# Nine products of constants ahead of the first operands, a first load on another queue, and the last statistics on another engine

## The chip, the cores and the metric

The kernel runs on one core of a Trainium2 chip. The metric is the device time of one execution in microseconds (us). "Before" is the median of three runs; one execution of the same kernel was recorded with a profile. TensorE (PE) multiplies matrices, VectorE (DVE), ScalarE (ACT) and GpSimd (POOL) work element by element, SyncE (SP) issues nearly all the transfers (DMA).

## The reference, cut to what matters

The kernel computes one decoder layer for 1024 tokens of width 2048, in float32: an RMS norm, one input projection of 9224 columns, two groups of recurrent heads in chunked form, an output projection with a residual, a gated per-layer embedding, and a last RMS norm. The change touches the first load of x, the first products, and the end:

```python
u = rmsnorm(h, norm_w[l])
proj = jnp.einsum('bsd,dc->bsc', u, w_in[l])
...
h = h + jnp.einsum('bsc,cd->bsd', y, w_out[l])
e = jnp.einsum('bsr,rd->bsd', p[l], w_pe[l])
gate = jax.nn.sigmoid(jnp.einsum('bsd,de->bse', rmsnorm(h, pe_norm_w[l]), w_pg[l]))
h = h + gate * e
out = rmsnorm(h, final_norm_w)   # h * rsqrt(mean(h*h) + EPS) * w
```

## The kernel before, in words

The tokens are worked in two halves of 512. Every large product is made in three passes (`mm3`, lines 253 to 255): each operand is split into a high part and a rest, and high x high, high x rest and rest x high are added up in PSUM. A weight piece `raw` comes by DMA, ACT casts the high part (L119), DVE takes the rest (L120); three pieces are kept ahead of the products. For the first half, x comes transposed in tiles of two k rows each (`xt`), ACT makes the high part of u (L240) from it and the norm weights in `vec_sb`, DVE the rest (L241). So the first block of products needs, for each k from 0 to 15, both parts of u and of its weights.

At the start SP issues, in this order: the first half of the first x tile (L75), the vector of constants `vec_sb` (L76), then weight parts (L167) and x tiles (L222, L224) in turn. ACT begins with loading its function table and makes `ones_r`, a rounded copy of the constant matrix `ones` (L86), which DVE has filled (L84). A program that lays out the order of the instructions on each engine works from simulated times (`schedule_with_timeline_sim=True`), so instructions don't all stand in the order of the source.

At the end `gate_block` makes the last column block (cb = 3) of the second half: token tiles 0 and 1 first, then 2 and 3 (prefix "b"), and the last token tile in two halves of 256 columns. For each piece ACT takes the sigmoid (L785), DVE multiplies by the embedding (L786) and adds the residual (L792), ACT squares and sums (L795) into a column of `ss3`. After the second half of a token tile DVE adds the five columns (L800), scales and adds EPS (L124), POOL raises to -1/2 (L125, `rstd_of`), ACT scales column blocks 0 and 2 (L809), DVE 1 and 3 (L807, L805), and SP issues the four stores of 256 KB each (L810).

Of the kernel before, what the change touches and what calls it, by code (L numbers as in the profile page):

```python
# [16 lines left out]
F32 = mybir.dt.float32  # L17
# [3 lines left out]
AF = mybir.ActivationFunctionType  # L21
ALU = mybir.AluOpType
AX = mybir.AxisListType

P = 128
S = 1024
D = 2048
KT = D // P
HT = 512
NC = HT // P  # L30
EPS = 1e-6
# [5 lines left out]
NMASK = 3 + len(LEVELS)  # L37
WIDE = (10, 16, 24)
HOLD = 2
LATE = [f"bg1_3_{pc}" for pc in (1, 3, 5, 7)]  # L40

V_NORM, V_PEN, V_MLN, V_HGN, V_LB, V_CW, V_CB, V_END = 0, 16, 32, 40, 48, 64, 96, 104
# [3 lines left out]
def hybrid_layer(ctx: ExitStack, tc, x, xT, pT, w_blk, w_v0, w_vw, w_out, w_pg, w_pe, vec, gb, fnw,  # L46
                 ident_in, causal_in, lmask_in, out):
    nc = tc.nc
# [9 lines left out]
    small = ctx.enter_context(tc.tile_pool(name="small", bufs=3))  # L58
    pj = ctx.enter_context(tc.tile_pool(name="pj", bufs=4, space=PS))
    mx = ctx.enter_context(tc.tile_pool(name="mx", bufs=4, space=PS))  # L60
# [5 lines left out]
    def psj(name):  # L66
        return pj.tile([P, 512], F32, tag="pj", name=name)

    def psm(name):
        return mx.tile([P, 512], F32, tag="mx", name=name)  # L70
# [1 line left out]

    vec_sb = const.tile([P, V_END], F32, name="vec_sb")
    x0 = mix.tile([P, 2, HT], F32, tag="at", name="xt0_0")
    nc.sync.dma_start(out=x0[:, 0], in_=xT[0:P, 0:HT])  # L75
    nc.sync.dma_start(out=vec_sb, in_=vec)  # L76
    ident = const.tile([P, P], F32, name="ident")
    causal = const.tile([P, P], F32, name="causal")
# [2 lines left out]
    neghalf = const.tile([P, 8], F32, name="neghalf")  # L81
    nc.vector.memset(neghalf, -0.5)
    ones = const.tile([P, P], F32, name="ones")
    nc.vector.memset(ones, 1.0)  # L84
    ones_r = orpool.tile([P, P + 112], F32R, name="ones_r")[:, 0:P]
    nc.scalar.copy(out=ones_r, in_=ones)  # L86

# [34 lines left out]
    def rstd_of(ss, n, width, name, tag="rstd"):  # L122
        r = small.tile([P, width], F32, tag=tag, name=name)
        nc.vector.tensor_scalar(out=r, in0=ss, scalar1=1.0 / n, scalar2=EPS, op0=ALU.mult, op1=ALU.add)  # L124
        nc.gpsimd.tensor_tensor(out=r, in0=r, in1=neghalf[:, 0:width], op=ALU.pow)  # L125
        return r
# [24 lines left out]
    def next_piece(between=None):  # L151
        nm, src = w_order[len(w_tiles)]
        n = src.shape[1] * src.shape[2]
        raw = wpool.tile([P, WP], F32, tag="wraw", name=f"raw_{nm}")[:, 0:n]
        if nm in LATE:
            hl = [upool.tile([P, 2, HT], F32R, tag="u", name=f"hl_{nm}_{i}") for i in range(2)]
# [16 lines left out]
    def load_piece(name):  # L173

        while len(w_tiles) < len(w_order) and (len(w_tiles) < AHEAD or w_order[len(w_tiles) - AHEAD][0] != name):
            next_piece()
        return dict(w_tiles[-AHEAD - 4:])[name]
# [74 lines left out]
    def mm3(ps, ah, al, bh, bl, first, last):  # L252
        nc.tensor.matmul(ps, lhsT=ah, rhs=bh, start=first, stop=False)  # L253
        nc.tensor.matmul(ps, lhsT=ah, rhs=bl, start=False, stop=False)  # L254
        nc.tensor.matmul(ps, lhsT=al, rhs=bh, start=False, stop=last)  # L255
# [432 lines left out]
    for half in range(2):  # L688
# [14 lines left out]
        for cb in range(4):  # L703
# [10 lines left out]
            for t in range(NC):  # L714
                tt = half * NC + t
# [5 lines left out]
                jk = tl.tile([P, 512], BF16, tag="junk2", bufs=1, name=f"jk2{half}_{cb}_{t}")  # L721
# [3 lines left out]
            for j in range(4):  # L725
                k = cb * 4 + j
                pt = psm(f"pht{half}_{k}")
                for t in range(NC):
# [5 lines left out]
                                               op0=ALU.mult, op1=ALU.subtract)  # L734
# [4 lines left out]
        ss3 = small.tile([P, NC, 5], F32, tag="ss3", bufs=1, name=f"ss3_{half}")  # L739
        nc.vector.memset(ss3, 0.0)  # L740
        h2 = [[None] * 4 for t in range(NC)]
        def gate_block(cb, ts_, pref):

            cs = slice(cb * 512, (cb + 1) * 512)
            wpe = load_piece(f"{pref}e{half}_{cb}")
            pe_sb = {}
            for t in ts_:
                pe = psm(f"pe{half}_{cb}_{t}")
                for kk in range(2):
                    ts = slice(kk * HT + t * P, kk * HT + (t + 1) * P)  # L750
                    sl = slice(kk * 512, (kk + 1) * 512)
                    mm3(pe, pp[:, 0, ts], pp[:, 1, ts], wpe[:, 0, sl], wpe[:, 1, sl], kk == 0, kk == 1)
                pe_sb[t] = pe

            units = []
            for t in ts_:
                parts = 2 if pref == "b" and t == NC - 1 else 1
                w = 512 // parts
                units += [(t, slice(i * w, (i + 1) * w), psj(f"pg{half}_{cb}_{t}_{i}")) for i in range(parts)]
            hold = HOLD if pref == "b" else 8  # L760
            hls = []
            for pc in range(8):
                hl = load_piece(f"{pref}g{half}_{cb}_{pc}")
                for kk in range(2):
                    sl = slice(kk * 512, (kk + 1) * 512)
                    hls.append([hl[kk][:, i] if isinstance(hl, list) else hl[:, i, sl] for i in range(2)])
                if pc < hold:
                    order = [(pc * 2 + kk, un) for kk in range(2) for un in units]
                elif pc == 7:
                    order = [(k, un) for un in units for k in range(2 * hold, KT)]  # L770
                else:
                    continue
                for k, (t, cl, ps) in order:
                    ts = slice(t * P, (t + 1) * P)
                    mm3(ps[:, cl], hns[k][:, 0, ts], hns[k][:, 1, ts], hls[k][0][:, cl], hls[k][1][:, cl],
                        k == 0, k == KT - 1)
            fb = tl.tile([P, 512], F32, tag="fb", bufs=1, name=f"fb{pref}{half}_{cb}")
            nc.sync.dma_start(out=fb, in_=fnw[:, cs].broadcast_to([P, 512]))
            for t, cl, ps in units:
                tt = half * NC + t  # L780
                if cl.start == 0:
                    hr = xh.tile([P, 512], F32, tag="xr", name=f"hr{half}_{cb}_{t}")
                    nc.sync.dma_start(out=hr, in_=h_dram[tt][:, cs])
                    gt = xh.tile([P, 512], F32, tag="ht", name=f"gt{half}_{cb}_{t}")
                nc.scalar.activation(out=gt[:, cl], in_=ps[:, cl], func=AF.Sigmoid, scale=r2[:, t:t + 1])  # L785
                nc.vector.tensor_tensor(out=gt[:, cl], in0=pe_sb[t][:, cl], in1=gt[:, cl], op=ALU.mult)  # L786
                if h2[t][cb] is None:
                    h2t = upool.tile([P, 2, HT], F32, tag="u", name=f"h2_{half}_{cb}_{t}")
                    c0 = cb - cb % 2
                    h2[t][c0], h2[t][c0 + 1] = h2t[:, 0], h2t[:, 1]  # L790
                hh = h2[t][cb]
                nc.vector.tensor_tensor(out=hh[:, cl], in0=gt[:, cl], in1=hr[:, cl], op=ALU.add)  # L792
                jk = tl.tile([P, 512], BF16, tag="junk2", bufs=1, name=f"jk3{half}_{cb}_{t}_{cl.start}")
                col = cb + (cl.start > 0)
                nc.scalar.activation(out=jk[:, cl], in_=hh[:, cl], func=AF.Square, accum_out=ss3[:, t, col:col + 1])  # L795
                if cb < 3:
                    nc.vector.tensor_tensor(out=hh, in0=hh, in1=fb, op=ALU.mult)
                elif cl.stop == 512:
                    s1 = small.tile([P, 1], F32, tag="s1", name=f"s1_{half}_{t}")
                    nc.vector.tensor_reduce(out=s1, in_=ss3[:, t], axis=AX.X, op=ALU.add)  # L800
                    r3 = rstd_of(s1, D, 1, f"r3_{half}_{t}")
                    for c in range(4):
                        ho = h2[t][c]
                        if c == 3:
                            nc.vector.scalar_tensor_tensor(out=ho, in0=ho, scalar=r3, in1=fb, op0=ALU.mult, op1=ALU.mult)  # L805
                        elif c == 1:
                            nc.vector.tensor_scalar(out=ho, in0=ho, scalar1=r3, scalar2=None, op0=ALU.mult)  # L807
                        else:
                            nc.scalar.activation(out=ho, in_=ho, func=AF.Copy, scale=r3)  # L809
                        nc.sync.dma_start(out=out[tt * P:(tt + 1) * P, c * 512:(c + 1) * 512], in_=ho)  # L810

        for cb in range(4):
            if half == 1 and cb == 3:
                gate_block(cb, (0, 1), "a")
                gate_block(cb, (2, 3), "b")
            else:
                gate_block(cb, range(NC), "")
# [81 lines left out]
```

## Time and profile before

| what | value |
|---|---|
| median of 3 runs | 2372.8 us (2372.53 to 2372.96) |
| the profiled execution | 2372.51 us, span 2370.5 us |
| PE busy | 2355.8 us, 99% of the span |
| DVE, ACT, POOL busy | 1170.9, 765.8, 66.3 us |
| granted TensorE clock, mean | 0.999 |
| DMA | 287.42 MB, mean 121 GB/s |

The span runs from the first instruction to the last on the profile's clock; the execution's time has 2.0 us around it. In rows of the timeline the columns are start, duration, engine, line, operation, output and inputs, shape, and how often; in brackets stands how long the engine had been idle and what released it. A matmul's recorded duration contains its way through the array: the step from one start to the next is what it costs in a row of them.

### The profile page before, as it was taken

The page shows a single profiled execution, that of the slowest core. Times are in us where ns is not written, and L with a number is a line of the kernel's source. Part 1 is how long each engine was busy: PE and PEld are TensorE (multiplying, and loading weights), DVE is VectorE, ACT ScalarE, POOL GpSimd, SP SyncE. Part 2 cuts the span into 40 slices and gives each one's busy share as a digit, 9 for nine tenths or more (in the row PEclk, how much of TensorE's full clock was granted, in tenths as well). Part 3 has the DMA queues.
Part 4 walks back from the last instruction along what each step waited for, and adds up shares of the span by engine and source line. Part 5 has one row for each costly group of instructions (what it writes and reads, how often), then busy time and mean ns, then how long its engine had stood idle before and what let it go on. Part 6 is the DMA issues. An engine that isn't in the chain of part 4 may idle for free.

```text
span 2370.5 us, 28577 instructions
## 1 busy us (share of the span) xinstructions
PE 2355.8 (99%) x11548; PEld 1984.1 (84%) x11548; DVE 1170.9 (49%) x1657; ACT 765.8 (32%) x1211; POOL 66.3 (3%) x96
## 2 busy tenths in 40 slices
PE   9999999999999999999999999999999999999998
PEld 7898888888888898988888888888888888888887
DVE  6655254265556857343534563675433444333336
ACT  6433232222222434232322222241423334332235
POOL 0000000000000000000000000000000000000000
PEclk9999999999999999999999999999999999999999
DMA  8433332322222423333333222343444456444436
GB/s 322 140 99 107 97 101 87 107 82 88 83 96 90 151 72 116 92 113 98 99 115 98 80 82 88 89 147 125 138 125 133 133 157 221 140 153 134 120 117 217
DMA packets 93452, 287.42 MB, mean 121 GB/s; under 512 B 10872, under 2 KB 11640, under 8 KB 93320
## 3 DMA queue, kind: packets, MB, share of 16 engines
q1 hardware_dynamic: 88200, 268.82, 36.5%
q0 software_dynamic: 5120, 16.78, 1.8%
q8 instruction: 90, 1.47, 0.3%
q14 instruction: 42, 0.34, 0.0%
HBM read 260.36 MB, written 25.20 MB: 120 GB/s over the span
## 4 chain that ended last, share of the span: by engine, by line
PE 99%; DMA 0%; DVE 0%; SPq 0%; ACT 0%; issue 0%; ACTq 0%; POOLq 0%
PE pj L254 15%; PE pj L253 15%; PE pj L255 15%; PE pt L253 5%; PE pt L255 5%; PE pt L254 5%; PE po L253 5%; PE pg L253 5%; PE po L255 5%; PE pg L254 5%; PE po L254 5%; PE pg L255 5%; PE pl L594 2%; PE pe L255 1%; PE pe L254 1%; PE pe L253 1%
## 5 line engine op out<-in xcount | busy, mean ns | idle before, releaser
L253 PE MATMUL pj<-u,hl 128*128 128x512 f32 x1536 | 603.5, 394 | 5.3 <-ACT hl L119 5.3
L254 PE MATMUL pj<-u,hl 128*128 128x512 f32 x1536 | 602.4, 392 | 0.1
L255 PE MATMUL pj<-u,hl 128*128 128x512 f32 x1536 | 601.2, 392 | 0.0
L120 DVE TENSOR_TENSOR hl<-raw,hl 128x1024 fp32r<-128x1024 f32 (+2 forms) x259 | 313.7, 1212 | 449.2 <-ACT hl L119 448.4
L119 ACT CAST hl<-raw 128x1024 fp32r<-128x1024 f32 (+2 forms) x259 | 269.4, 1040 | 819.8 <-PE pj L255 554.1
L253 PEld LDWEIGHTS pj<-u,hl 128*128 128x128 f32 x1536 | 288.8, 188 | 64.8 <-ACT hl L119 5.3
L254 PEld LDWEIGHTS pj<-u,hl 128*128 128x128 f32 x1536 | 289.1, 188 | 59.9 <-DVE u L241 0.9
L255 PEld LDWEIGHTS pj<-u,hl 128*128 128x128 f32 x1536 | 289.0, 188 | 59.6 <-issue 0.2
L254 PE MATMUL pt<-hl,u 128*128 128x512 f32 (+2 forms) x640 | 223.7, 350 | 0.0
L253 PE MATMUL pt<-hl,u 128*128 128x512 f32 (+2 forms) x640 | 222.9, 349 | 0.5 <-DVE raw L385 0.5
L255 PE MATMUL pt<-hl,u 128*128 128x512 f32 (+2 forms) x640 | 221.9, 348 | 0.0
L253 PE MATMUL po<-hl_o,ys 128*128 128x512 f32 x512 | 200.5, 393 | 0.0
L254 PE MATMUL po<-hl_o,ys 128*128 128x512 f32 x512 | 200.0, 391 | 0.0
L255 PE MATMUL po<-hl_o,ys 128*128 128x512 f32 x512 | 199.4, 390 | 0.0
L253 PE MATMUL pg<-hl_g,hnt 128*128 128x512 f32 x448 | 174.9, 390 | 0.0
L254 PE MATMUL pg<-hl_g,hnt 128*128 128x512 f32 x448 | 174.5, 390 | 0.0
L255 PE MATMUL pg<-hl_g,hnt 128*128 128x512 f32 x448 | 174.3, 389 | 0.0
L120 DVE TENSOR_TENSOR hl_o<-raw_o,hl_o 128x1024 fp32r<-128x1024 f32 x64 | 78.4, 1225 | 153.9 <-ACT hl_o L119 153.9
L120 DVE TENSOR_TENSOR hl_g<-raw_g,hl_g 128x1024 fp32r<-128x1024 f32 x56 | 68.6, 1225 | 167.4 <-ACT hl_g L119 167.4
L253 PEld LDWEIGHTS pt<-hl,u 128*128 128x128 f32 x640 | 120.6, 189 | 15.7 <-issue 0.8
L254 PEld LDWEIGHTS pt<-hl,u 128*128 128x128 f32 x640 | 120.8, 189 | 14.9 <-issue 0.2
L255 PEld LDWEIGHTS pt<-hl,u 128*128 128x128 f32 x640 | 120.5, 189 | 15.0 <-issue 0.2
(263 smaller groups left out, 2638.4 us busy)
## 6 DMA issues: line engine op xcount, KB each, us to landing
raw<-in_w_blk_dram SPq DMA_DIRECT2D x199, 512.0 KB, 3.9
raw_o<-in_w_out_dram SPq DMA_DIRECT2D x64, 512.0 KB, 3.7
raw_g<-in_w_pg_dram SPq DMA_DIRECT2D x56, 512.0 KB, 3.7
raw<-in_w_vw_dram SPq DMA_DIRECT2D x48, 512.0 KB, 3.6
yr<-y SPq DMA_DIRECT2D x32, 256.0 KB, 4.2
xr<-in_x_dram SPq DMA_DIRECT2D x32, 256.0 KB, 5.7
h<-ht POOLq DMA_DIRECT2D x32, 256.0 KB, 6.2
hr<-h SPq DMA_DIRECT2D x32, 256.0 KB, 3.7
```

The costliest lines, as they stand in the source:

```text
L119: nc.scalar.copy(out=dst_hi, in_=src)
L120: nc.vector.tensor_tensor(out=dst_lo, in0=src, in1=dst_hi.bitcast(F32), op=ALU.subtract)
L253: nc.tensor.matmul(ps, lhsT=ah, rhs=bh, start=first, stop=False)
L254: nc.tensor.matmul(ps, lhsT=ah, rhs=bl, start=False, stop=False)
L255: nc.tensor.matmul(ps, lhsT=al, rhs=bh, start=False, stop=last)
L594: nc.tensor.matmul(pl[0:M, c * 64:(c + 1) * 64], lhsT=kf[:, c * P:c * P + M], rhs=qv[:, c * nb:(c + 1) * nb, 1, :], start=True, stop=True)
```

## The change

Ahead of everything else on TensorE stand nine products of the constant matrix `ones` with itself (128x128, float32) into a PSUM tile that nothing reads. The first half of the first x tile is issued by ACT instead of SP. For the last piece (the second 256 columns of the last token tile) the sum of squares is taken by DVE; the columns of the sum that are known after the first 256 columns are added up ahead (`sp`, one [128, 2] tile), so that after the last sum of squares one operation gives mean + EPS instead of two. The store of column block 2 of that token tile is issued by ACT instead of SP.

```diff
+WARM = 9
...
     x0 = mix.tile([P, 2, HT], F32, tag="at", name="xt0_0")
-    nc.sync.dma_start(out=x0[:, 0], in_=xT[0:P, 0:HT])
+    nc.scalar.dma_start(out=x0[:, 0], in_=xT[0:P, 0:HT])
     nc.sync.dma_start(out=vec_sb, in_=vec)
...
+    warm = mx.tile([P, 512], F32, tag="mx", name="warm")
+    for i in range(WARM):
+        nc.tensor.matmul(warm[:, 0:P], lhsT=ones, rhs=ones, start=True, stop=True)
...
-                nc.scalar.activation(out=jk[:, cl], in_=hh[:, cl], func=AF.Square, accum_out=ss3[:, t, col:col + 1])
+                if cl.start > 0:
+                    nc.vector.tensor_tensor_reduce(out=gt[:, cl], in0=hh[:, cl], in1=hh[:, cl], scale=1.0, scalar=0.0,
+                                                   op0=ALU.mult, op1=ALU.add, accum_out=ss3[:, t, col:col + 1])
+                else:
+                    nc.scalar.activation(out=jk[:, cl], in_=hh[:, cl], func=AF.Square, accum_out=ss3[:, t, col:col + 1])
+                if cl.stop == 256:
+                    sp = small.tile([P, 2], F32, tag="sp", name=f"sp_{half}_{t}")
+                    nc.vector.tensor_reduce(out=sp[:, 0:1], in_=ss3[:, t, 0:4], axis=AX.X, op=ALU.add)
+                    nc.vector.tensor_scalar(out=sp[:, 1:2], in0=sp[:, 0:1], scalar1=1.0 / D, scalar2=EPS, op0=ALU.mult,
+                                            op1=ALU.add)
...
                 elif cl.stop == 512:
-                    s1 = small.tile([P, 1], F32, tag="s1", name=f"s1_{half}_{t}")
-                    nc.vector.tensor_reduce(out=s1, in_=ss3[:, t], axis=AX.X, op=ALU.add)
-                    r3 = rstd_of(s1, D, 1, f"r3_{half}_{t}")
+                    if cl.start > 0:
+                        r3 = small.tile([P, 1], F32, tag="rstd", name=f"r3_{half}_{t}")
+                        nc.vector.scalar_tensor_tensor(out=r3, in0=ss3[:, t, 4:5], scalar=1.0 / D, in1=sp[:, 1:2],
+                                                       op0=ALU.mult, op1=ALU.add)
+                        nc.gpsimd.tensor_tensor(out=r3, in0=r3, in1=neghalf[:, 0:1], op=ALU.pow)
+                    else:
+                        (the two steps as before)
...
-                        nc.sync.dma_start(out=out[tt * P:(tt + 1) * P, c * 512:(c + 1) * 512], in_=ho)
+                        q = nc.scalar if cl.start > 0 and c == 2 else nc.sync
+                        q.dma_start(out=out[tt * P:(tt + 1) * P, c * 512:(c + 1) * 512], in_=ho)
```

## Rows read from the trace of the kernel before

**Rows 1.** The waits of PE from 14.6 to 2361 us: total, times, longest.

```profile
PE pt L253 <- DVE raw L385: 0.5, 1, 0.5
```

**Rows 2.** The timeline of the start, all engines.

```profile
0.74 1.28 ACT L86 ACT_TABLE_LOAD   x1 [0.74 <-PEq L889]
...
0.74 0.38 SPq L75 DMA_DIRECT2D xt<-in_xT_dram  x1
...
0.87 0.17 DVE L84 MEMSET ones<- 128x128 f32 x1
...
1.18 0.42 SPq L76 DMA_DIRECT2D vec_sb<-in_vec_dram  x1
...
4.20 0.72 ACT L240 ACTIVATE u<-xt,vec_sb 128x512 fp32r<-128x512 f32 x1 [1.87 <-DMA vec_sb<-in_vec_dram]
```

**Rows 3.** The timeline of PE's first products, from 5 to 15 us.

```profile
5.26 1.22 PE L253 MATMUL pj<-u,hl 128*128 128x512 f32 x2 [5.26 <-ACT hl L119]
...
8.85 1.05 PE L254 MATMUL pj<-u,hl 128*128 128x512 f32 x2
...
9.70 1.05 PE L255 MATMUL pj<-u,hl 128*128 128x512 f32 x2
...
10.80 0.74 PE L253 MATMUL pj<-u,hl 128*128 128x512 f32 x2
...
14.57 0.19 PEld L254 LDWEIGHTS pj<-u,hl 128*128 128x128 f32 x1 [0.40 <-DVE u L241]
```

**Rows 4.** The chain of waits from 0 to 30 us: start, duration, what.

```profile
4.01 5.99 DMA xt<-in_xT_dram
...
10.78 0.76 DVE u L241
...
12.08 0.23 PE pj L255
```

**Rows 5.** The timeline of ACT and DVE from 11.5 to 16 us.

```profile
11.54 1.05 ACT L119 CAST hl<-raw 128x1024 fp32r<-128x1024 f32 x1 [0.18 <-DMA raw<-in_w_blk_dram]
...
12.63 1.22 DVE L120 TENSOR_TENSOR hl<-raw,hl 128x1024 fp32r<-128x1024 f32 x1 [0.44 <-ACT hl L119]
...
13.77 2.73 DVE L241 SCALAR_TENSOR_TENSOR u<-xt,vec_sb,u 128x512 fp32r<-128x512 f32 x4
```

**Rows 6.** The timeline of the end, from PE's last product.

```profile
2361.61 0.47 ACT L785 ACTIVATE gt<-pg,r 128x256 f32<-128x256 f32 x1 [1.14 <-PE pg L255]
...
2362.57 0.43 DVE L792 TENSOR_TENSOR h<-gt,hr 128x256 f32<-128x256 f32 x1
...
2363.09 0.42 ACT L795 ACTIVATE jk<-h 128x256 bf16<-128x256 f32 x1 [1.01 <-DVE h L792]
...
2363.63 0.16 DVE L800 TENSOR_REDUCE s<-ss 128x1 f32<-128x5 f32 x1 [0.64 <-ACT jk L795]
...
2363.83 0.15 DVE L124 TENSOR_SCALAR r<-s 128x1 f32<-128x1 f32 x1
...
2364.15 0.54 POOL L125 TENSOR_TENSOR r<-r,neghalf 128x1 f32<-128x1 f32 x1 [5.45 <-DVE r L124]
...
2364.73 1.33 ACT L809 ACTIVATE h<-h,r 128x512 f32<-128x512 f32 x2 [1.13 <-POOL r L125]
```

**Rows 7.** SP's last stores, from its timeline.

```profile
2365.24 1.80 SPq L810 DMA_DIRECT2D out_dram<-h  x4
```

**Rows 8.** Busy time by window: PE, PEld, DVE, ACT, POOL, granted clock, DMA share, GB/s.

```profile
2364.00:2366.00 2.00, 0.00 (x0) 0.00 (x0) 1.15 (x2) 1.27 (x2) 0.54 (x1) 0.99 0.00 0
...
2366.00:2368.00 2.00, 0.00 (x0) 0.00 (x0) 0.00 (x0) 0.06 (x1) 0.00 (x0) 0.50 0.98 367
```

**Rows 9.** The chain of waits at 51 us: one float32 product of 512 columns.

```profile
51.37 0.87 PE rb L204 x2
```

**Rows 10.** The timeline of DVE at 27 us: a sum of squares taken by DVE.

```profile
26.92 1.22 DVE L193 CUSTOM_DVE_ANT_0 xs<-xs 128x1024 f32<-128x1024 f32 x1
...
28.06 0.09 DVE L193 DVE_READ_ACCUMULATOR2_ANT ssx<- 128x1 f32 x1
```

More of the change, by code (lines that the diff above doesn't have):

```diff
@@ L798, in gate_block @@
                 elif cl.stop == 512:
-                    s1 = small.tile([P, 1], F32, tag="s1", name=f"s1_{half}_{t}")
-                    nc.vector.tensor_reduce(out=s1, in_=ss3[:, t], axis=AX.X, op=ALU.add)
-                    r3 = rstd_of(s1, D, 1, f"r3_{half}_{t}")
+                    if cl.start > 0:
[4 more added lines that the diff above has]
+                    else:
+                        s1 = small.tile([P, 1], F32, tag="s1", name=f"s1_{half}_{t}")
+                        nc.vector.tensor_reduce(out=s1, in_=ss3[:, t], axis=AX.X, op=ALU.add)
+                        r3 = rstd_of(s1, D, 1, f"r3_{half}_{t}")
                     for c in range(4):
```

## The prediction

> **What bounds the kernel now.** I read the page first, then the waits of PE, then only the two ends of the span. The page puts PE at 2355.8 us of 2370.5, and from 14.6 us to the last product PE waits for another engine once, 0.5 us long [rows 1]. So a change can pay in three places only: before PE is dense (the first 14.6 us), after its last product (2361.6 us on), and in that one wait.
>
> At the start SP issues the first x tile at 0.74 us and the constants `vec_sb` at 1.18 us; every later load stands behind these two on SP. The first piece of u starts at 4.20 us, when `vec_sb` lands [rows 2]. PE starts at 5.26 us. Its first products go at the lower of its two clock levels: two products take 9.70 - 8.85 = 0.85 us, 0.425 us each, which for 512 columns is 1.2 GHz [rows 3]; two us later the step is 0.23 us, the 2.4 GHz level [rows 4]. The low level therefore ends at about 10.8 us, some 5.5 us after PE began. But what holds PE is not the clock. The products of k = 0 and 1 are twelve, 5.26 + 12 x 0.425 = 10.4 us at the low level; those of k = 2 start at 10.80 us, as soon as ACT has made its u. The chain of waits leads from there to an x tile issued at 4.01 us that landed 5.99 us later, and on to DVE's rest of u [rows 4]. The last wait of the start is at 14.57 us, 0.40 us for DVE's rest of u of k = 4 [rows 3]: that operation starts at 13.77 us on DVE, right behind the rest of a weight piece (12.63), which follows ACT's cast (11.54), which waited for a transfer [rows 5]. After that PE is its own limit. So what the start is worth is how much earlier that chain of transfers comes.
>
> At the end a chain of single operations runs: residual added at 2362.57, ACT's squares at 2363.09, two small DVE operations, POOL's power at 2364.15, scaling from 2364.73 [rows 6], then four stores on SP in 1.80 us [rows 7], whose data move from about 2366 us on with the DMA engines 98% busy at 367 GB/s [rows 8].
>
> **The change part by part: the start.** *The x tile to ACT's queue.* SP is rid of its first issue, so `vec_sb` is issued where the x tile was: 1.18 - 0.74 = 0.44 us earlier [rows 2], and everything behind it on SP with it (weight parts, x tiles), since up to 4.01 us SP issues without a pause. I take 0.44 us for the chain to 14.57 us. Bounds: 0, if the engines are what limits the landing, up to 0.9 us, if also the share of the first tile's traffic falls away from SP's queue and as much is gained again. The x tile itself is issued by ACT at 0.74 us, ahead of the table load; that load moves from 0.74 to about 1.15 and ends at 2.4 us, covered, since ACT's first u starts at 3.8 us at the earliest. If instead the tile's issue stood behind the table load (1.28 us), u of k = 0 would come 1.3 us later; that too is covered by the wait before k = 2.
>
> *Nine products of constants.* A float32 product of 512 columns takes 0.87 us at the high level [rows 9], so one of 128 columns 0.22 us, and at the low level (0.425 / 0.23 as long) 0.41 us: nine take at most 3.7 us. `ones` is filled at 1.04 us [rows 2], so they run from about 1.2 to 4.9 us. The first real product was at 5.26 us and comes to 4.82 us by the 0.44: PE may start it 0.1 us late. If the level rises after no longer a stretch of products than before, it is up by 6.7 us, and the products of k = 0 and 1, which wait for their own operands between, end at about 8.2 us instead of 10.75. Then PE waits for u of k = 2, at 10.80 - 0.44 = 10.36 us. So I cost the products at nothing and give them nothing: the 2.4 us that the higher clock saves go into a longer wait, because the load of x hides all of it. If that cover were gone they would be worth these 2.4 us. Their PSUM tile is one of four of its kind and is free again after the ninth.
>
> Here a rule speaks against the change. The row: PE's last product ends at 2361.6 us [rows 6], and the granted clock still stands at 0.99 of full in 2364 to 2366 us and at 0.50 after it [rows 8], so it holds for some 4.4 us without work; the new gap is 2.2 us. The Trainium skill ("TensorE: Matmul & The Clock Gate", section "HAM oscillation — how this bites in real kernels") says that waits between bursts of products can put the clock back, so that each next burst starts at the low level. By the row the sum keeps its 0.44 us; by the rule taken at its worst it would lose some 1.9 us here.
>
> **The end.** *Squares on DVE.* Before, POOL starts 2364.15 - 2362.57 = 1.58 us after the residual's start. After: residual 0.43 us, and 0.04 us from one small DVE operation to the next (2363.63 + 0.16 to 2363.83) [rows 6]. The sum of squares by DVE took 1.22 us for 1024 columns [rows 10], as much as a plain DVE operation of 1024 [rows 5]; the plain one of 256 takes 0.43 us [rows 6], so I take 0.43 us; its reading of the accumulator starts 0.08 us before that ends and takes 0.09 us [rows 10]. Then 0.04 us, one operation in place of two, and POOL 0.32 us after that one's start (2363.83 to 2364.15). Sum: 0.43 + 0.04 + 0.35 + 0.09 + 0.04 + 0.32 = 1.27 us, a gain of 0.31 us. Bounds: 0.40 us, if the reading is hidden; a loss of 0.48 us, if the 256 columns cost what 1024 do. The two `sp` operations cost 0.3 us of DVE while PE still works on the last products; nothing waits for them.
>
> *One store on ACT.* SP's four stores take 0.45 us apiece; ACT's takes the last one's turn away, so all are issued 0.45 us earlier relative to the first. But the four are 4 x 262 KB = 1.05 MB, at 367 GB/s 2.9 us, longer than the issuing. The end is set by the first store and the bandwidth, and nothing stands behind the store on ACT. I take 0.05 us, bounds 0 and 0.45.
>
> **The sum.** 0.44 + 0 + 0.31 + 0.05 = 0.80 us off the profiled execution's 2372.51 us: 2371.7. The median of the runs shown is 0.3 us above it, so for a median 2372.8 - 0.8 = 2372.0 us, 0.03% less. About 0.2%, 4.7 us, is what a measurement of this kernel can tell from no change.
>
> **The rivals.** *The transfers come no earlier.* The x tile now moves at the same time as `vec_sb` and the first weights; if they share what there is, `vec_sb` lands where it did. For it: later, from 8 us on, PE's waits end on landings and not on issues. Against it: from 0.74 to past 4.01 us SP issues one load behind the other, so up to there the engines get work only as fast as SP hands it out [rows 2, 4]. Head 0: 2372.8 - 0.36 = 2372.4 us. The Trainium skill ("DMA: Bandwidth & Descriptors", section "Issuing engines are not separate DMA queues") has it that another issuing engine saves the time of issuing and nothing else; whether that time counts is what the rival disputes.
>
> *The clock falls in the gap.* Place: between k = 1 and k = 2, about 8.2 to 10.4 us. Price 0.425 - 0.23 = 0.2 us a product, for as many as at first, twelve, 2.4 us, less the slack that PE has until 14.57 us (3.77 us for fourteen products of 0.23 us: 0.55). 1.85 us above the forecast, 2373.9 us, slower than before. It takes four products at the low level beyond the slack to end above before, and some thirty to end 0.2% above.
>
> *The order comes out otherwise.* All instructions are laid out by simulated times, and the start is moved. Place: the product of L204, on which the one wait hangs [rows 1]. Each product of 0.23 us that stands before it instead of behind it costs 0.23 us; put earlier, it gains 0.5 us at most. With four more before it the kernel is slower than before, with about 24 by 0.2%. Elsewhere weights are split three pieces ahead, some 5 us of products a piece, which covers a moved split. 2371.5 to 2374 us; most likely nothing.
>
> *The end doesn't do what it says:* DVE's sum of squares at its upper bound gives back 0.79 us: 2372.8 us.
>
> **How the numbers follow.** Forecast (2371.6 to 2372.3 us) 0.58; no earlier transfers 0.14; clock falls 0.08; other order 0.14; slow end 0.06. The range takes in the bounds of the start and of the end and part of the order: 2371.2 (0.9 at the start, 0.7 at the end) to 2373.6, and leaves out the clock's 2373.9 and the worse half of the order. Faster by over 0.2% would want 4.7 us, and the three places together hold less that this change reaches: 0.01. Slower by as much only from a bad order or a clock that stays low for thirty products: 0.03. The same: 0.96.
>
> **What would show it.** Right: nine products from about 1.2 us; the first u at about 3.8 us; PE's steps at 0.23 us before 8 us; an idle gap of about 2 us before k = 2; the last wait for u of k = 4 at about 14.1 us; no ACT squares in the last chain and POOL 1.27 us after the residual. Wrong: a step of 0.425 us after 10.4 us; x tiles landing where they did; a wait of PE in the middle that isn't there now; a changed time from PE's last product to the end by other than 0.3 to 0.4 us.

## The result and the profile after

The changed kernel is slower. Its median is 2385.11 us (2384.35 to 2386.05, five runs; a sixth, at a granted clock of 0.75, is left out), against 2372.88 us for the kernel before (2372.53 to 2373.10, six runs): ratio 1.0052 [1.0038, 1.0066], 12.2 us more. The prediction said 2372.0 us and a range up to 2373.6. The profiled execution took 2384.84 us with a span of 2382.8 us, 12.3 us more than before's span, at the same mean granted clock, 0.999. What follows splits these 12.3 us.

The waits of PE in the changed kernel, over the whole span; columns: total, times, longest.

```profile
PE pj L258 <- ACT u L245: 1.4, 1, 1.4
PE warm L89 <- DVE mcar L110: 1.1, 1, 1.1
PE pt L258 <- DVE raw L390: 0.5, 1, 0.5
```

The wait ahead of k = 2 is there, shorter than forecast. The one in the middle is the old one [rows 1], unchanged. So the order did not turn bad, and behind the start PE waits for nothing new: 12 us were lost by an engine that is always busy.

The start, from the timeline of the changed kernel, all engines.

```profile
0.74 0.41 ACTq L76 DMA_DIRECT2D xt<-in_xT_dram  x1
0.74 0.38 SPq L77 DMA_DIRECT2D vec_sb<-in_vec_dram  x1
...
1.09 4.14 PE L89 MATMUL warm<-ones 128*128 128x128 f32 x18 [1.09 <-DVE mcar L110]
...
1.18 1.28 ACT L91 ACT_TABLE_LOAD   x1 [1.18 <-PEq L910]
...
4.19 0.71 ACT L245 ACTIVATE u<-xt,vec_sb 128x512 fp32r<-128x512 f32 x1
```

PE's first products in the changed kernel, from its timeline.

```profile
5.24 0.73 PE L258 MATMUL pj<-u,hl 128*128 128x512 f32 x2
...
6.42 0.63 PE L260 MATMUL pj<-u,hl 128*128 128x512 f32 x2
6.88 0.62 PE L258 MATMUL pj<-u,hl 128*128 128x512 f32 x2
...
7.79 0.61 PE L260 MATMUL pj<-u,hl 128*128 128x512 f32 x2
9.79 0.73 PE L258 MATMUL pj<-u,hl 128*128 128x512 f32 x2 [1.38 <-ACT u L245]
...
13.44 0.47 PE L259 MATMUL pj<-u,hl 128*128 128x512 f32 x1
```

The nine products end at 5.23 us and hold up nothing: ACT has the first weights ready at 5.2 us. From 6.42 us on two products take 0.46 us, the higher level, where before they took 0.85 until 10.8 us [rows 3]. The 27th product of x (L259, u of k = 4) starts at 13.44 us; the same one started at 14.57 us before [rows 3]. At this point the changed kernel is 1.13 us ahead.

The end, from the timeline of the changed kernel, all engines.

```profile
2374.22 0.47 ACT L790 ACTIVATE gt<-pg,r 128x256 f32<-128x256 f32 x1 [1.00 <-PE pg L260]
...
2375.19 0.42 DVE L797 TENSOR_TENSOR h<-gt,hr 128x256 f32<-128x256 f32 x1
2375.65 0.42 DVE L801 CUSTOM_DVE_ANT_0 gt<-h 128x256 f32<-128x256 f32 x1
2376.00 0.08 DVE L801 DVE_READ_ACCUMULATOR2_ANT ss<- 128x1 f32 x1
2376.11 0.16 DVE L815 SCALAR_TENSOR_TENSOR r<-ss,sp 128x1 f32<-128x1 f32 x1
2376.44 0.54 POOL L817 TENSOR_TENSOR r<-r,neghalf 128x1 f32<-128x1 f32 x1 [4.99 <-DVE r L815]
...
2378.39 0.38 ACTq L831 DMA_DIRECT2D out_dram<-h  x1
```

From the residual's start to POOL it is 2376.44 - 2375.19 = 1.25 us (1.27 forecast, 1.58 before [rows 6]); from the last sigmoid to POOL 2.22 us against 2.54. From POOL to the end of the span it is 6.36 us against 2370.5 - 2364.15 = 6.35, which is the same: the spans are given to 0.1 us. So the shorter sum of squares does what it was said to do, and the store on ACT shows no gain.

Neither end has the loss, so it lies in between. The windows of the kernel before show it, one of the output projection and one of the gate stage; columns as in [rows 8], with the number of instructions in brackets.

```profile
1700.00:1800.00 100.00, 100.00 (x461) 82.96 (x460) 34.83 (x39) 30.45 (x45) 5.35 (x9) 1.00 0.46 145
1800.00:1900.00 100.00, 100.00 (x443) 82.81 (x442) 37.82 (x43) 30.68 (x43) 0.00 (x0) 1.00 0.41 122
```

The same windows of the changed kernel.

```profile
1700.00:1800.00 100.00, 100.00 (x461) 82.88 (x460) 34.83 (x39) 30.45 (x45) 5.35 (x9) 1.00 0.45 145
1800.00:1900.00 100.00, 100.00 (x429) 80.40 (x428) 36.28 (x42) 29.73 (x42) 0.00 (x0) 1.00 0.38 116
```

PE is 100% busy in all four at a granted clock of 1.00, and yet from 1800 to 1900 us it gets through 429 products instead of 443: 100 / 443 = 0.226 us a product before, 100 / 429 = 0.233 after. In the window ahead of it the counts are equal. A busy share and a clock can't show this; the count can. Which products are slower is seen in the groups by line, with shapes kept apart. The kernel before:

```profile
L253 PE MATMUL po<-hl_o,ys 128*128 128x512 f32 x512 | 200.5, 393 | 0.0
...
L253 PE MATMUL pg<-hl_g,hnt 128*128 128x512 f32 x448 | 174.9, 390 | 0.0
...
L538 PE MATMUL cs_d<-hl_d,ones_r 128*128 128x512 f32 x16 | 6.2, 389 | 0.0
```

The changed kernel:

```profile
L258 PE MATMUL pj<-u,hl 128*128 128x512 f32 x1536 | 602.9, 394 | 1.4 <-ACT u L245 1.4
...
L258 PE MATMUL po<-hl_o,ys 128*128 128x512 f32 x512 | 200.6, 393 | 0.0
...
L258 PE MATMUL pg<-hl_g,hnt 128*128 128x512 f32 x448 | 178.1, 398 | 0.0
...
L543 PE MATMUL cs_d<-hl_d,ones_r 128*128 128x512 f32 x16 | 6.3, 397 | 0.0
```

The products `pj` and `po` keep their mean of 394 and 393 ns, `pg` goes from 390 to 398; `pe`, not shown, from 389 to 397, and the few `cs` products of the mixing stage by 4 to 8 ns. All are of the same shape and type. Their code and number are the same in both kernels. The 96 `pg` products of 256 columns, not shown, did not slow down (282 ns before, 280 after).

The bookkeeping of the span, from places that both traces have: the 27th product of x is 1.13 us earlier; from there to the last transposes of the mixing stage (`hpt`, 1681.29 us before, 1681.66 after) 1.50 us are lost; from these to the last sigmoid (2361.61 and 2374.22 us) 12.24 us; the end gives 0.32 back. -1.13 + 1.50 + 12.24 - 0.32 = 12.3 us. The gate stage has 1488 products `pg` and 192 `pe` of 512 columns: 12.24 us / 1680 = 7.3 ns each.

### The profile page after: what moved, and what is told of

It is laid out like the page before. It is cut to its first block, busy times and chain, and to the rows that moved or that the text cites. A ratio compares the mean times of both kernels' runs of the same rounds, so it can differ in the third digit from the quotient of the medians.

```text
span 2382.8 us, 28613 instructions
## 1 busy us (share of the span) xinstructions
PE 2371.2 (100%) x11566; PEld 1987.7 (83%) x11566; DVE 1171.6 (49%) x1660; ACT 765.6 (32%) x1209; POOL 66.9 (3%) x96
## 4 chain that ended last, share of the span: by engine, by line
PE 99%; DMA 0%; DVE 0%; SPq 0%; ACT 0%; issue 0%; POOLq 0%
PE pj L259 15%; PE pj L258 15%; PE pj L260 15%; PE pg L260 5%; PE pg L258 5%; PE pg L259 5%; PE pt L258 5%; PE pt L259 5%; PE pt L260 5%; PE po L258 5%; PE po L259 5%; PE po L260 5%; PE pl L599 2%; PE pe L259 1%; PE pe L258 1%; PE pe L260 1%
## 5 line engine op out<-in xcount | busy, mean ns | idle before, releaser
L259 PE MATMUL pj<-u,hl 128*128 128x512 f32 x1536 | 601.9, 392 | 0.1
L259 PEld LDWEIGHTS pj<-u,hl 128*128 128x128 f32 x1536 | 288.5, 188 | 59.7 <-DVE u L246 1.0
L259 PE MATMUL pt<-hl,u 128*128 128x512 f32 (+2 forms) x640 | 224.0, 350 | 0.0
L259 PE MATMUL po<-hl_o,ys 128*128 128x512 f32 x512 | 200.2, 391 | 0.0
L258 PE MATMUL pg<-hl_g,hnt 128*128 128x512 f32 x448 | 178.1, 398 | 0.0
L259 PE MATMUL pg<-hl_g,hnt 128*128 128x512 f32 x448 | 177.8, 397 | 0.0
L260 PE MATMUL pg<-hl_g,hnt 128*128 128x512 f32 x448 | 177.6, 396 | 0.0
L259 PEld LDWEIGHTS pt<-hl,u 128*128 128x128 f32 x640 | 120.8, 189 | 15.0 <-issue 0.2
```

## The experiments

**What could slow a product by 3%.** The new tile `sp` is two floats wide and has three buffers; in the compiled kernel each takes 32 bytes of every partition, 96 in all. Every tile that is allocated behind the small ones lies 96 bytes further on: those of the mixing stage and, in the last stage, `hnt` and `pp`. The weights `hl_g` and `hl_e` lie ahead of them and stay. In `pg` and `pe` the moved tiles are the stationary operands and the weights the moving ones; in `cs` the moving operand `hl_s`, `hl_d` moved and the stationary `ones_r` did not; in `pj` and `po` neither did. In the kernel before, all these operands start at addresses that leave the same remainder, 128, when divided by 256 bytes; in the changed one the moved tiles leave 224. So the theory: the step of a product depends on the place of its two operands in SBUF. The rivals: the new operations or the new order do it, or it is enough for a tile to lie on a multiple of some size by itself, or ACT and DVE, which write the next weights meanwhile, meet the moved reads. The last one the trace answers: in the changed kernel the step of `pg` is 0.234 us where ACT or DVE works beside it (781 products) and where neither does (537), before 0.227 us in both cases.

**e1: `sp` with four buffers**, 128 bytes in place of 96, on the changed kernel.

```diff
-sp = small.tile([P, 2], F32, tag="sp", name=f"sp_{half}_{t}")
+sp = small.tile([P, 2], F32, tag="sp", bufs=4, name=f"sp_{half}_{t}")
```

> The whole change, but the new small tile sp gets four buffers instead of three, so that it takes 128 bytes of each partition and not 96; everything behind it in SBUF moves by 128 bytes. Theory (the 96 bytes moved the tiles hnt and pp, which TensorE loads as stationary operands in the last stage, off a multiple of 128 bytes, and each product on them steps 0.234 instead of 0.227 us): the step of the pg products is back at 0.227 us, and the time is before less the gains at both ends, 2371.2 to 2371.8 us. Rival (the order of the instructions or the PSUM bank, turned by one by the tile of the nine products, makes them slow): as the changed kernel, about 2385 us.

Measured 2383.32 us (2382.69 to 2383.44), before on the same chip 2373.0: 1.0044 [1.0027, 1.0061]. The mean of `pg` is 396, 395, 395 ns. A shift by 128 bytes is nearly as bad as one by 96: the expectation that it would bring the step back fell.

**e2, e3, e4, e6, e7: the kernel before with an unused tile behind the small ones**, of 96, 32, 64, 512 and 256 bytes per partition (N), filled once by POOL. Nothing else is changed, so it has neither the new order nor the new operations.

```diff
     small = ctx.enter_context(tc.tile_pool(name="small", bufs=3))
+    padp = ctx.enter_context(tc.tile_pool(name="padp", bufs=1)).tile([P, N // 4], F32, name="padp_t")
...
+    nc.gpsimd.memset(padp, 0.0)
```

> The kernel before with nothing of the change but an unused tile of 96 bytes a partition behind the small tiles (GpSimd fills it once at the start). Theory of the address: pg products step 0.234 us, the time is before plus 12 to 14 us, 2385 to 2387 us. Rival (order or PSUM bank): as before, 2372.9 us.

Measured 2386.52 us (2385.97 to 2389.66): 1.006 [1.0045, 1.0075].

> As the one with 96 bytes, but 32 bytes. If what counts is being a multiple of 64 or 128 bytes, the same 12 to 14 us above before; if the remainder counts in proportion, some 4 us or another amount. Rival (order or bank): 2372.9 us.

Measured 2385.29 us (2384.85 to 2385.57): 1.0052 [1.0037, 1.0067].

> As the one with 96 bytes, but 64 bytes. If a multiple of 64 bytes is enough: 2372.9 us, as before. If it must be a multiple of 128: some 12 us above. This run tells the two apart; the rival of order or bank has 2372.9 us here too.

Measured 2384.19 us (2383.64 to 2384.58): 1.0047 [1.0032, 1.0062]. The three ran beside the same 2373.0 us as e1.

> The kernel before with an unused tile of 512 bytes behind the small tiles; steps of 32, 64 and 96 bytes cost 11 to 14 us. If the place counts by a period of 512 bytes: 2372.9 us, as before. If it counts by a longer period or by the exact place: slower by some us.

Measured 2373.41 us (2372.45 to 2374.58), before 2373.49: 1.0 [0.9991, 1.001].

> As the one with 512 bytes, but 256. If the period is 256 bytes or less: 2372.9 us. If it is 512: about 10 us above before, as with 128 bytes in the whole change.

Measured 2373.06 us (2372.25 to 2374.24): 0.9997 [0.9988, 1.0006].

The group of `pg` by line, e4 (64 bytes):

```profile
L255 PE MATMUL pg<-hl_g,hnt 128*128 128x512 f32 x448 | 177.8, 397 | 0.0
```

and e7 (256 bytes):

```profile
L255 PE MATMUL pg<-hl_g,hnt 128*128 128x512 f32 x448 | 175.0, 391 | 0.0
```

An unused tile alone costs what the whole change cost. So the loss is shown to come from where the tiles lie, and not from an operation or the order. It comes back to nothing at 256 and 512 bytes; 32, 64, 96 and 128 cost 10 to 14 us, in no clear order.

**e5 and e15: the whole change with the places of before.** The buffer of `ones_r`, ahead of the small tiles, has a tail of 112 unused floats; 24 fewer make up for the 96 bytes, so that the tiles behind `sp` lie where they lay. e15 is the same kernel a second time, on another chip.

```diff
-    ones_r = orpool.tile([P, P + 112], F32R, name="ones_r")[:, 0:P]
+    ones_r = orpool.tile([P, P + 88], F32R, name="ones_r")[:, 0:P]
```

> The whole change, with the unused tail of the tile ones_r cut by 96 bytes, so that all tiles behind the small ones stand at the very addresses of before (hnt, pp and the others). Theory (the place of hnt and pp in SBUF makes the last stage slow): step of the pg products 0.227 us, time 2371.2 to 2371.8 us. Rival (order or PSUM bank as well): above 2375 us.

Measured 2371.72 us (2370.97 to 2374.75, ten runs), before 2373.49: 0.9995 [0.9986, 1.0005].

> The refitted whole change again, beside the two others. Both theories: 2371.0 to 2371.8 us and 2374.3 to 2374.8 us, about half of the runs each.

Measured 2372.51 us (2370.94 to 2373.37, eleven runs), before 2373.09: 0.9997 [0.9988, 1.0006].

The loss is gone with 24 floats that nothing reads. What is left, 1.8 and 0.6 us less than before, can't be told from no change, nor from the 0.8 us of the prediction: both intervals take in 1. The expectation of e15, half of the runs at 2374.3 us or more, failed: none of the eleven is there.

**e8 and e9: is it a tile's own place, or that of the two operands to each other?** On the kernel before: 96 unused bytes ahead of all tiles (e8: all operands move together), or 96 ahead of the weights' buffers and 160 behind these (e9: the weights move by 96, all that is behind them by 256, which e7 showed to be harmless). The line below stands ahead of the first pool in e8 and behind `upool` in e9, which has another of 40 floats behind `hlpool`.

```diff
+    padp = ctx.enter_context(tc.tile_pool(name="padp", bufs=1)).tile([P, 24], F32, name="padp_t")
```

> The kernel before with 96 unused bytes ahead of all tiles, so that stationary and moving operands of all large products move together by 96 bytes. Theory A (what counts is where the stationary operand stands relative to the moving one): 2372.9 us, as before. Theory B (what counts is the place of the stationary operand in itself): all 10,000 large products step 7 ns longer, about 70 us above before.

Measured 2372.93 us (2372.21 to 2376.26), before 2373.49: 0.9998 [0.9988, 1.0008].

> The kernel before with 96 unused bytes ahead of the weight tiles hl and 160 behind them, so that of all operands hl alone changes its place relative to the others (the rest moves by 0 or 256 bytes, which cost nothing). hl is the moving operand of pt, po, pg and pe and the stationary one of pj. Theory A (the two operands' places relative to each other, by 256 bytes): every large product, some 10,000, steps 6 to 7 ns longer, 2433 to 2445 us. Theory C (it has to do with hnt and pp and something else than hl, such as what ACT, DVE or DMA do beside): as before, 2373 us.

Measured 2432.06 us (2431.89 to 2433.48), before 2373.09: 1.0249 [1.0233, 1.0266], 59 us more. Groups by line in e9:

```profile
L257 PE MATMUL pj<-u,hl 128*128 128x512 f32 x1536 | 613.9, 401 | 5.5 <-ACT hl L123 5.2 <-ACT u L244 0.4
...
L257 PE MATMUL po<-hl_o,ys 128*128 128x512 f32 x512 | 204.2, 400 | 0.0
```

Here the products that had kept their step lose it: `pj` 394 to 401 ns, `po` 393 to 400. In its timeline 0.47 us go by from the first of three to the third, 0.235 apiece:

```profile
30.54 0.40 PE L257 MATMUL pj<-u,hl 128*128 128x512 f32 x1
30.77 0.40 PE L258 MATMUL pj<-u,hl 128*128 128x512 f32 x1
31.01 0.39 PE L259 MATMUL pj<-u,hl 128*128 128x512 f32 x1
```

The products of 512 columns (4608 `pj`, 1152 `pt`, 1536 `po`, 1488 `pg` and 192 `pe`) share 59 us: 6.6 ns each; the 768 `pt` products of 256 and 264 columns keep their mean within 2 ns. The time is 1 us below the range of theory A, 59 us above that of C: A holds and C falls. What counts is the place of stationary and moving operand to each other, in all such products of 512 columns, and not where either lies.

One group seems not to fit. In e9 both operands of `cs` moved by 256 bytes, and yet the mean of `cs_d` goes from 389 to 393 and 394 ns. But a slow step carries over to the products behind it, as the changed kernel shows, where `cs` is slow and `pj` is not:

```profile
499.08 0.39 PE L258 MATMUL pj<-u,hl 128*128 128x512 f32 x1
...
499.76 0.40 PE L543 MATMUL cs_d<-hl_d,ones_r 128*128 128x512 f32 x1
500.00 0.40 PE L544 MATMUL cs_d<-hl_d,ones_r 128*128 128x512 f32 x1
500.23 0.40 PE L258 MATMUL pj<-u,hl 128*128 128x512 f32 x1
500.46 0.40 PE L259 MATMUL pj<-u,hl 128*128 128x512 f32 x1
500.70 0.39 PE L260 MATMUL pj<-u,hl 128*128 128x512 f32 x1
500.93 0.39 PE L258 MATMUL pj<-u,hl 128*128 128x512 f32 x1
```

Ahead of `cs_d` the three `pj` take (499.76 - 499.08) / 3 = 0.227 us each, from there on five products take (500.93 - 499.76) / 5 = 0.234, three of them `pj`, of which neither operand moved. In e9 `cs` stands among slow `pj` and `pt` in the same way; that this is its whole loss there was not tested.

**e10, e11, e12: the parts alone, at the places of before.** e10 has the start (nine products, and the x tile on ACT), e11 the nine products alone, both on the kernel before; e12 is the whole change at the old places without these two. The diff is that of e10; e11 has only its lower half.

```diff
-    nc.sync.dma_start(out=x0[:, 0], in_=xT[0:P, 0:HT])
+    nc.scalar.dma_start(out=x0[:, 0], in_=xT[0:P, 0:HT])
...
+    warm = mx.tile([P, 512], F32, tag="mx", name="warm")
+    for i in range(9):
+        nc.tensor.matmul(warm[:, 0:P], lhsT=ones, rhs=ones, start=True, stop=True)
```

> The nine products and the x tile on ACT's queue, with the end as before; no tile in SBUF moves. Changed kernel's profile: the last wait of the start came 1.13 us earlier. If both parts stay as they are: 1.1 us below before. If only the 0.44 us of the first issue count, as predicted: 0.44 us below.

Measured 2371.81 us (2371.32 to 2374.07), before 2373.09: 0.9997 [0.9988, 1.0006].

> The nine products alone, the x tile issued by SP as before. As predicted they are worth nothing, since k = 2 waits for its x tile: within 0.1 us of before; the last wait of the start (PE's products of k = 4) at 14.4 to 14.6 us of the span. Rival (the faster first products let weights and u follow sooner): some 0.5 us below.

Measured 2374.24 us (2372.82 to 2376.47): 1.0004 [0.9996, 1.0013]. Its eleven runs lie in two groups, five from 2372.8 to 2373.2 us and six from 2374.2 to 2376.5.

> The end alone (squares on DVE, sp, store on ACT), start as before, the tail of ones_r cut by 96 bytes so that no operand moves. From PE's last product to POOL 0.30 us less and the store on ACT 0.05 us: 0.35 us below before. Rival (the store on a second queue is worth its 0.4 us of issue): 0.7 us below.

Measured 2372.45 us (2371.95 to 2372.7): 0.9997 [0.9988, 1.0006].

None can be told from no change. The upper runs of e11, and those of e5 (four of ten above 2372.9 us), raise the question of the gap ahead of k = 2. The profiled run of e5 was one of them; its PE timeline:

```profile
10.22 0.73 PE L258 MATMUL pj<-u,hl 128*128 128x512 f32 x2 [2.04 <-ACT u L245]
...
12.39 1.05 PE L258 MATMUL pj<-u,hl 128*128 128x512 f32 x2
13.24 0.63 PE L259 MATMUL pj<-u,hl 128*128 128x512 f32 x1
...
15.45 0.39 PE L259 MATMUL pj<-u,hl 128*128 128x512 f32 x1
```

and its windows (granted clock third from the right):

```profile
10.00:12.00 2.00, 1.72 (x6) 1.11 (x7) 1.42 (x2) 1.54 (x3) 0.00 (x0) 0.90 1.05 387
12.00:14.00 2.00, 2.00 (x6) 1.62 (x5) 1.68 (x2) 1.62 (x3) 0.00 (x0) 0.50 1.03 411
14.00:16.00 2.00, 2.00 (x8) 1.55 (x8) 2.00 (x4) 1.98 (x4) 0.00 (x0) 0.74 1.05 404
```

After a gap of 2.04 us the clock fell to 0.50 (1.2 GHz), and the steps are 0.43 us. From the first product of k = 2 to the 27th product it takes 15.45 - 10.22 = 5.23 us; in the changed kernel 13.44 - 9.79 = 3.65. The fall costs 1.6 us where it happens; the prediction's rival had it at 1.85.

The fall isn't all of it. In the same run of e5 PE waits once more, for the weights of the last piece:

```profile
PE pg L258 <- ACT hl_bg L124: 0.4, 1, 0.4
PE pg L259 <- DVE hl_bg L125: 0.4, 2, 0.2
```

From the last transposes to the last sigmoid it takes 2364.11 - 1682.18 = 681.93 us there, against 2361.61 - 1681.29 = 680.32 before: 1.6 us more. Nor is the fall new: on the chip of e5 7 of the 31 runs of the kernel before have a mean granted clock of 0.998 instead of 0.999 and take 2373.8 to 2374.8 us. On the chip of e10 and e11 none of the runs before has it, and four of eleven in each of these two do.

**e13: the gap filled**, at the old places: eight more products of constants behind those of k = 1.

```diff
+                    if half == 0 and b == 0 and k == 1 and i == 1:
+                        with tc.issue_after(m.ins):
+                            for _ in range(8):
+                                nc.tensor.matmul(warm[:, 0:P], lhsT=ones, rhs=ones, start=True, stop=True)
```

> The refitted whole change, with eight more products of constants right behind the products of k = 1, where TensorE stands idle 1.4 to 2.2 us. Theory (the gap makes the clock fall in part of the runs): steps of 0.23 us from 7 us on, no run in the upper group, median 2371.4 us. Rival (the two groups come from the transfers, not from the clock): two groups as before, part of the runs at about 2374.4 us.

Measured 2372.58 us (2371.12 to 2373.26, eleven runs), before 2373.09: 0.9997 [0.9988, 1.0006]. Its PE timeline:

```profile
8.65 1.95 PE L275 MATMUL warm<-ones 128*128 128x128 f32 x16
10.51 0.73 PE L258 MATMUL pj<-u,hl 128*128 128x512 f32 x2
```

The gap is gone, all eleven runs have a mean granted clock of 0.999, and none lies in an upper group. But its median is not the 2371.4 us of the expectation, and it isn't faster than e15, which ran beside it without the filling: e15 had no upper group either, so what the filling is worth stays open.

**e14: the store back on SP**, at the old places.

```diff
-                        q = nc.scalar if cl.start > 0 and c == 2 else nc.sync
+                        q = nc.sync
```

> The refitted whole change with the last store of column block 2 issued by SP again. As predicted (the stores are bound by bandwidth): 0.05 us above the refitted change in the faster group. Rival (the store on ACT saves its turn on SP): 0.4 us above.

Measured 2371.87 us (2370.8 to 2373.3), before 2373.09: 0.9995 [0.9987, 1.0004]; e15 beside it 2372.51. From POOL's power to the end of the span it is 6.40 us, with the store on ACT 6.34 (e15) and 6.37 (e5), by spans that are given to 0.1 us. The instructions' own times, which are finer, give 6.36 us (e14), and 6.36 to 6.42 us in all eleven profiles with the store on SP; in the six with it on ACT they give 6.38 to 6.39. So the move of the store shows no gain.

## Why the prediction was wrong

- **The step that failed** is the last sentence on the end: "The two `sp` operations cost 0.3 us of DVE while PE still works on the last products; nothing waits for them." The operations cost just that. The tile behind them was not costed: its 96 bytes moved the stationary operands of 1680 products against their moving operands, 7.3 ns each, 12.2 us. An unused tile of the same size does it alone (e2), and taking 96 bytes away elsewhere undoes it (e5, e15). With it fell the assumption that carries the whole working, that the change pays "in three places only" since "after that PE is its own limit": PE was, and its limit moved. No rival of the prediction has this mechanism; to slower by over 0.2% it gave 0.03.
- **The mixing stage** lost 1.50 us between the 27th product and the last transposes. In all profiles with the tiles at their old places to each other, or moved by 256 or 512 bytes, this stretch is within 0.2 us of before's 1666.7; in the five with the tiles moved by 32 to 128 bytes it is 1.1 to 1.7 us longer. Of the changed kernel's 1.50 us the steps of the 80 `cs` products are 0.49 and those of the five products behind each of them 0.61, by the carrying over shown with e9; where the remaining 0.4 us come from is open.
- **The x tile on ACT: 0.44 us, not refuted.** SP issues `vec_sb` at 0.74 us as forecast. The first u still starts at 4.19 us and not at 3.8, since ACT now takes the small operation of L102 first; that stands ahead of the wait for k = 2 and costs nothing. Before k = 2, ACT's u starts at 9.61 us in the mean of seven profiles with the tile on ACT and at 10.21 in that of ten with it on SP: 0.60 us, while single profiles reach from 9.02 to 9.88 and from 9.57 to 11.33. That is too wide to tell 0.44 from 0.60, and the changed kernel's 1.13 us is one draw of it; e15's 27th product starts at 14.54 us, as before's.
- **Nine products: nothing, right in the changed kernel's profile.** They took 4.14 us and not "at most 3.7", the level is up by 6.4 us, and PE waits for k = 2 instead. Alone (e11) they came out 1.15 us above before, which can't be told from no change, with a fallen clock in part of the runs.
- **The rule on gaps and its rival (0.08): real, but not the cause.** The changed kernel's gap was 1.38 us, and its clock did not fall; it fell after gaps of 2.04 (e5), 2.23 (e10) and 2.75 us (e2), and not after 1.60 (e14), 1.76 (e15) and 1.83 (e11). The Trainium skill ("TensorE: Matmul & The Clock Gate", section "HAM oscillation — how this bites in real kernels") says that waits between bursts can put the clock back; these traces show it both ways, at a price of 1.6 us. The prediction's row for the other side, the clock held for 4.4 us behind the last product, did not carry over to the start.
- **Squares on DVE: 0.31 us forecast, 0.32 measured. Store on ACT: 0.05 forecast, none measured** (6.36 to 6.42 us on SP, 6.38 to 6.39 on ACT). The Trainium skill ("DMA: Bandwidth & Descriptors", section "Issuing engines are not separate DMA queues") has another issuing engine save the issuing alone; here not even that shows, as the prediction's lower bound of 0 had it.
- **The sum** of 0.80 us off stands against 1.8 and 0.6 us (e5, e15) for the change at the old places, both too small for a measurement to tell from nothing. What the edits do in time agrees with the profiles, but for the store; what they do in space was left out.

Open: why the place matters. That a shift of one operand by 256 or 512 bytes costs nothing, and that both moving together costs nothing, is shown; why, and whether reads of the two meet, was not tried. Why 32, 64, 96 and 128 bytes cost different amounts, and why products of 256 columns kept their step, is open too. Open as well is why the weights `hl_bg` of the last piece come late in some runs: in the profiles of e5 and e14 PE waits for them, and the last stage takes 1.6 and 1.3 us longer than before's.

## What to carry to other kernels

A new tile, however small, moves all that is allocated behind it: where one engine is always busy, compare the addresses of its operands before and after a change, and keep stationary and moving operands at their places to each other (here, a shift by 256 or 512 bytes did no harm). When the time moves and no wait does, count the instructions in equal windows, and compare the mean of one by shape: busy shares and the clock say nothing. And test an edit at the old addresses before judging it; 24 floats of padding decided here between 12 us lost and nothing lost.

## What the runs showed of the hardware

- The step of a matmul of 512 columns with float32 operands in the reduced form (fp32r) was 0.226 to 0.227 us with both operands' addresses at the same remainder by 256 bytes, and 0.232 to 0.235 us after one of the two had been moved by 32, 64, 96 or 128 bytes; moves by 256 and 512 changed nothing. Moving the weights alone by 96 bytes cost this kernel 59 us, 2.5%, at an unchanged granted clock and with no wait added.
- A slow step carries over: behind two slow products (`cs_d`) three of another kind (`pj`), with unmoved operands, took 0.233 us each, before 0.227.
- An element of the layout that computes nothing can be worth more than every edit of the change: the tail of `ones_r` at 112 floats and at 88.
- The granted clock's record can be 1.00 where the steps are those of 1.2 GHz: from 5.2 to 10.8 us before [rows 3] the windows give 1.00. In the first microseconds the step is the safer reading.
